# Norm sums gathered with the output blocks instead of from the updated residual, in a two-layer hybrid decoder step

## The chip, the cores and the metric

The kernel runs on one core of a Trainium2 chip. The metric is device time in microseconds (us) of one execution, as the median of several runs. The engines are named as the profile names them: PE multiplies matrices (PEld loads its weights), DVE is the vector engine, ACT the scalar engine, POOL is GpSimd, SP issues the transfers.

## The reference, cut to what matters

One inference step of two trunk layers, for 512 prompt tokens and 64 sample tokens together (576 columns). Each layer is a feed-forward network (FFN), a token mixer and a second FFN. The first layer's mixer is a state-space mixer with a gated linear unit (GLU), the second's is a latent attention. Every one of the six sublayers is wrapped by two norms:

```python
def rms_norm(x, g):
    y = x * rsqrt(mean(x * x, axis=-1, keepdims=True) + 1e-6)
    return y * g

h = f(rms_norm(x, norm_pre))            # f: FFN, state-space mixer or attention
x = x + w * rms_norm(h, norm_post)      # w is 1/2 for an FFN, 1 for a mixer
```

So the norm in front of a sublayer needs the sum of squares of an x that the norm behind the sublayer before has just changed. Width is 1024, the FFN's inner width 2816, everything is float32.

## The kernel before, in words

Activations stand transposed: 128 partitions by 8 blocks k of the width, by 576 columns in two halves h of 288 (`hs(h)`). X is the residual, Y the output of a sublayer, R the factor of the norm in front (one number per column, spread over all partitions), ACC the sum of squares by partition. A product is done with operands split in a high and a low part, three matmuls per pair (`mm3`, L155 to L158); weights are split on ACT and DVE as they land (`split`, L149; `load`, L174); `xsplit` (L189) makes XH and XL from X for a sublayer's first product.

`stats` (L98) sums ACC over partitions on PE (L103), works out the inverse root in nine small operations on DVE (L107 to L116) and builds a diagonal `rs_d` (L117). `spread` (L124) multiplies it by ones on PE (L127), so that the factor stands on all partitions. `post` (L205) adds the normed output to X, block by block: one operation on DVE to make t, one addition on DVE or POOL, then `xsplit`. `squares` (L232) then takes the squares of the new X on ACT and adds them up on POOL.

`tail` (L247) is the end of every sublayer. Blocks 6 and 7 of half 0 are computed, half 0's output norm is worked out while block 6 of half 1 runs, and half 0's residual while block 7 of half 1 runs. Half 1's norm and residual are left in `state["pend"]`, and `first_units` (L262) of the next sublayer runs them between its matmuls: norm after k = 0, residual after k = 2. Then it sums ACC for half 0 (L275) and half 1 (L287) and spreads both into R; R is needed when the first products leave PSUM (`evac`).

The state-space mixer (`s5_mixer`, L622) has no such first product. It starts with `run_pend` (L645): all of half 1's residual, the squares of half 1 (L222 to L227), both norms D0 and D1. Then a pipeline of ten steps over eight blocks k follows: `s_u` scales X[:, k] by R into `un`, `s_a` and `s_b` transpose, `s_c` and `s_s` run the recurrence on products kept in pieces of Y (`wk`), `s_d` and `s_e` make the output. `zeros` (L649) clears some buffers on POOL, tied behind the last residual addition (L812).

The order within an engine is set before the run by a planner: it takes the instruction that comes first in the program among those it believes ready, by its own costs, and `issue_after` ties one behind another. Buffers are rings: "t1" has four, "sq" three.

Of the kernel before, what the change touches and what calls it, by code (L numbers as in the profile page):

```python
# [9 lines left out]
F32 = mybir.dt.float32  # L10
# [7 lines left out]
T = 576  # L18
# [7 lines left out]
def build(nc, tc, a, subs=(0, 1, 2, 3, 4, 5)):  # L26
# [9 lines left out]
    with ctx:  # L36
# [40 lines left out]
        ACC = cst.tile([128, T], F32, name="ACC")  # L77
        GP = cst.tile([128, 6, 2, 8], F32, name="GP")
# [19 lines left out]
        def stats(accs, col=None, scale=1.0, eps=1e-6):  # L98

            src = psum()[:CP, :4]  # L100
            for i, z in enumerate(accs):
                for j in range(4):
                    P.matmul(src[:, j:j + 1], z[:, j * CP:j * CP + CP], ones[:, 0:1] if col is None else col,  # L103
                             start=i == 0 and j == 0, stop=i == len(accs) - 1 and j == 3)
            q, t, y = [cur["sm"].tile([CP, 4], F32, name=nm) for nm in ("rs_a", "rs_t", "rs_y")]

            V.tensor_scalar(q, src, eps, None, op0=OP.add)  # L107
# [8 lines left out]
            V.scalar_tensor_tensor(y, t, 5.0, y, op0=OP.add, op1=OP.mult)  # L116
            d = smt("rs_d")[:CP]  # L117
            state["y"] = y
# [3 lines left out]
            return d  # L122

# [8 lines left out]
        def sqacc(acc, src, first, scale=1.0, defer=False, ve=False, add=None):  # L132
            if ve:
                sq = acc if first else smt("sq")
                V.tensor_tensor(sq, src, src, op=OP.mult)
                if not first:
                    G.tensor_tensor(acc, acc, sq, op=OP.add)
                return None
            if first:
                A.activation(acc, src, AF.Square, scale=scale)  # L140
                return None
            sq = sqd.tile([128, H], F32, name="sqd") if defer else smt("sq")
            ins = A.activation(sq, src, AF.Square, scale=scale)  # L143
            if defer:
                state["sqd"] = ins
                return sq
            (add or G).tensor_tensor(acc, acc, sq, op=OP.add)  # L147
# [56 lines left out]

        def post(n, h, rs, nxt):  # L205
            last = None
            for k in range(8):
                t = smt("t1")
                V.scalar_tensor_tensor(t, Y[:, k, hs(h)], GP[:, n, 1, k:k + 1], rs, op0=OP.mult, op1=OP.mult)  # L209
                ve = k % 2 if nxt in (None, 1) else k % 4 == 0  # L210
                ins = (V if ve else G).tensor_tensor(X[:, k, hs(h)], X[:, k, hs(h)], t, op=OP.add)  # L211
                last = last if ve else ins
                if nxt is None:
                    if k % 2:
                        S.dma_start(a["o_y"][:, k - 1:k + 1, hs(h)], X[:, k - 1:k + 1, hs(h)])
                elif nxt != 1:
                    xsplit(nxt, h, k)
            if nxt == 1 and h == 1:
                state["add"] = last
                s5["D0"] = stats([ACC[:, hs(0)]]), state["y"]  # L220
                sqs = []
                for k in range(8):  # L222
                    sqs.append(s5["sq"].tile([128, H], F32, name="sq%d" % k))
                    A.activation(sqs[k], X[:, k, hs(h)], AF.Square)
                for x, y in ((4, 5), (6, 7), (4, 6)):
                    V.tensor_tensor(sqs[x], sqs[x], sqs[y], op=OP.add)
                s5["D1"] = stats(sqs[:5]), state["y"]  # L227
            elif h == 1:
                squares(h, nxt, last)
            return last  # L230

        def squares(h, nxt, last):  # L232
            if nxt is not None:
                with tc.issue_after(last.ins), tc.issue_after(state["sqd"].ins):
                    for k in range(8):
                        sqacc(ACC[:, hs(h)], X[:, k, hs(h)], k == 0, add=G)

# [9 lines left out]
        def tail(n, blk, mlast, SQ, nxt):  # L247

            for m in mlast:
                blk(m, 0)  # L250
            d0 = stats([ACC[:, hs(0)], SQ[0]])
            blk(mlast[0], 1)
            if nxt not in (None, 1):
                state["W0"] = cur["load"](first(nxt, 0), 2048)
            last = post(n, 0, spread(d0), nxt)
            for m in mlast[1:]:
                blk(m, 1)
            squares(0, nxt, last)
            d1 = []
            state["pend"] = [lambda: d1.append(stats([ACC[:, hs(1)], SQ[1]])), lambda: post(n, 1, spread(d1[0]), nxt)]  # L260

        def first_units(W, evac, K=8):  # L262
# [12 lines left out]
            d0 = stats([ACC[:, hs(0)]])  # L275
            qq = [[], []]
            for u in range(2):
                for g in range(2):
                    qq[u].append(psum()[:, :H])
                    for k in range(K):  # L280
                        mmk(u, qq[u][g], 1, g, k)
                    if (u, g) == (0, 0):
                        spread(d0, R[:, hs(0)])
                        for v in range(2):
                            evac(v, 0, pp[v])
                    if (u, g) == (0, 1):
                        d1 = stats([ACC[:, hs(1)]])  # L287
            spread(d1, R[:, hs(1)])
# [14 lines left out]
        def ffn(i, n, nxt, tick=lambda *z: None):  # L303
# [7 lines left out]
            def evac(f, h, pp):  # L311
                t, s, u = smt("t1"), smt("t2"), smt("t3")
                V.tensor_tensor(t, pp[0], R[:, hs(h)], op=OP.mult)  # L313
                A.activation(s, t, AF.Silu)  # L314
                V.tensor_tensor(u, pp[1], R[:, hs(h)], op=OP.mult)  # L315
                g = G.tensor_tensor(u, u, s, op=OP.mult)  # L316
                tick(*split(HH[:, f, hs(h)], HL[:, f, hs(h)], u), g)

            if n == subs[0]:
# [9 lines left out]
                d0 = stats([ACC[:, hs(0)]])  # L329
# [3 lines left out]
                d1 = stats([ACC[:, hs(1)]])  # L333
# [19 lines left out]
            for s in range(2):  # L353
# [5 lines left out]
                def down(d, h):  # L359
# [6 lines left out]
                    if s == 0:  # L366
                        tick(A.activation(y, o, AF.Copy))
                    else:
                        ins = V.tensor_tensor(y, o, y, op=OP.add)  # L369
                        SQ[h] = sqacc(ACC[:, hs(h)], y, d == 0, defer=d == 7)  # L370
                        tick(ins)
# [250 lines left out]
        def s5_mixer(n, nxt, es_c):  # L622
# [13 lines left out]
            if n == subs[0]:  # L636
# [4 lines left out]
                for h in range(2):  # L641
                    s5["D%d" % h] = stats([ACC[:, hs(h)]]), state["y"]
            es_q = ExitStack()
            s5["sq"] = mkpool(es_q, "s5q", 1, reuse_waits="tile")
            run_pend()  # L645
            es_q.close()
# [11 lines left out]
            wk = lambda k, i: fl[:, (4 * (k % 2) + i) * 512:(4 * (k % 2) + i) * 512 + 512].rearrange("p (r g c) -> p r g c", r=2, g=4)  # L658
            UN, U2, WVt, RTt, TTt, YTt, MKt = {}, {}, {}, {}, {}, {}, {}

            def s_u(k):
# [6 lines left out]
                if k:  # L668
                    V.scalar_tensor_tensor(u, X[:, k], GP[:, n, 0, k:k + 1], R, op0=OP.mult, op1=OP.mult)
# [11 lines left out]
            def s_a(k):  # L681

                TT = TTt[k] = ep.tile([CP, 8, 8, 16], F32, name="TT")
                if k == 0:

                    u = UN[0]
                    for h in range(2):
# [77 lines left out]
            def s_e(k):  # L765
# [3 lines left out]
                for h in range(2):  # L769
# [3 lines left out]
                    y, w, sq = smt("t2"), smt("t3"), smt("sq")  # L773
# [22 lines left out]
            for s in range(10):  # L796
# [11 lines left out]
                if s == 0:  # L808
# [4 lines left out]
                    with tc.issue_after(state["add"].ins) if "add" in state else nullcontext():  # L813
                        zeros()
# [31 lines left out]
            def gevac(m, h, pp):  # L846
# [4 lines left out]
                SQ[h] = sqacc(ACC[:, hs(h)], y, m == 0, scale=0.5, defer=m == 7)  # L851
# [28 lines left out]
        def mla(n, nxt):  # L880
# [77 lines left out]
            for h in range(2):  # L958
                t, u = smt("t1")[:64], smt("t2")[:32]
# [104 lines left out]
            for u in range(6):  # L1064
# [5 lines left out]
                for h in range(2):  # L1070
# [3 lines left out]
                    if u < 2:  # L1074
                        t = [smt(nm) for nm in ("t1", "t2", "t3", "sq")]
# [67 lines left out]
            def evac(m, h, o):  # L1143
                A.activation(Y[:, m, hs(h)], o, AF.Copy)
                SQ[h] = sqacc(ACC[:, hs(h)], Y[:, m, hs(h)], m == 0, defer=m == 7)
# [14 lines left out]
            for m in range(2, 6):  # L1160
                for h in range(2):
                    blk(m, h)
# [393 lines left out]
```

## Time and profile before

| what | value |
|---|---|
| median of 3 runs | 2486.22 us (2485.14 to 2488.54) |
| profiled execution | 2486.95 us, span of its instructions 2485.2 us |
| PE busy | 2381.8 us, 96% of the span |
| DVE busy | 1281.5 us, 52% |
| ACT busy | 873.6 us, 35% |
| POOL busy | 556.1 us, 22% |
| mean granted clock of PE | 0.978 of 2.4 GHz |
| chain that ended last | PE 68%, DVE 6%, ACT 2%, POOL 1% |

Busy time is the union of an engine's instructions. The rows in a later section are of four kinds. A row of the waits names who waited, for whom, the us in total, how often, and the longest. A timeline row has the start in us from the span's start, the duration, the engine, the line of the kernel, the operation, output and inputs, shape, how many were merged, and in brackets the idle time before it and who ended it. A row of groups (lines) has busy us, the mean in ns, and idle us before. A row of windows has busy us (and number) for each engine in a stretch.

### The profile page before, as it was taken

The page shows a single profiled execution, that of the slowest core. Times are in us where ns is not written, and L with a number is a line of the kernel's source. Part 1 is how long each engine was busy: PE and PEld are TensorE (multiplying, and loading weights), DVE is VectorE, ACT ScalarE, POOL GpSimd, SP SyncE. Part 2 cuts the span into 40 slices and gives each one's busy share as a digit, 9 for nine tenths or more (in the row PEclk, how much of TensorE's full clock was granted, in tenths as well). Part 3 has the DMA queues.
Part 4 walks back from the last instruction along what each step waited for, and adds up shares of the span by engine and source line. Part 5 has one row for each costly group of instructions (what it writes and reads, how often), then busy time and mean ns, then how long its engine had stood idle before and what let it go on. Part 6 is the DMA issues. An engine that isn't in the chain of part 4 may idle for free.

```text
span 2485.2 us, 44160 instructions
## 1 busy us (share of the span) xinstructions
PE 2381.8 (96%) x17610; PEld 2313.1 (93%) x17610; DVE 1281.5 (52%) x2647; ACT 873.6 (35%) x1807; POOL 556.1 (22%) x819
## 2 busy tenths in 40 slices
PE   7999999789989999998999999899999999999998
PEld 7999999679989999998999999798888898999997
DVE  7564565685464233347432433767777655423434
ACT  4222322353332222224222222434666653222221
POOL 3123535452231001124100112530000042100112
PEclk9999999799989999998999999999999999999999
DMA  3224343473212222222223222345555332222221
GB/s 126 86 86 146 126 130 118 125 188 97 77 60 86 71 92 86 75 88 68 80 67 101 86 70 76 114 114 178 169 173 179 130 104 69 75 74 99 86 71 63
DMA packets 114642, 254.89 MB, mean 103 GB/s; under 512 B 25122, under 2 KB 53539, under 8 KB 114179
## 3 DMA queue, kind: packets, MB, share of 16 engines
q1 hardware_dynamic: 114434, 252.06, 32.0%
q8 instruction: 139, 2.28, 0.4%
q14 instruction: 69, 0.56, 0.1%
HBM read 231.79 MB, written 22.59 MB: 102 GB/s over the span
## 4 chain that ended last, share of the span: by engine, by line
PE 68%; DVE 6%; ACT 2%; issue 1%; POOL 1%; DMA 1%; SPq 0%; ACTq 0%; DVEq 0%; POOLq 0%
PE ps L158 20%; PE ps L156 20%; PE ps L157 20%; PE ps L1331 2%; PE ps L1296 2%; DVE XHL L153 1%; DVE t L209 1%; POOL X L211 1%; PE ps L127 1%; PE ps L1237 1%; DVE wlo L151 1%; PE ps L1317 0%; PE ps L757 0%; PE ps L1225 0%; ACT Pm L1198 0%
## 5 line engine op out<-in xcount | busy, mean ns | idle before, releaser
L156 PE MATMUL ps<-XHL,whi 128*128 128x288 f32 x3344 | 1002.4, 300 | 20.4 <-ACT whi L151 12.9
L157 PE MATMUL ps<-XHL,whi 128*128 128x288 f32 x3344 | 998.7, 299 | 4.7 <-DVE XHL L153 4.7
L158 PE MATMUL ps<-XHL,wlo 128*128 128x288 f32 x3344 | 995.9, 298 | 1.4 <-DVE wlo L151 1.4
L156 PEld LDWEIGHTS ps<-XHL,whi 128*128 128x128 f32 x3344 | 638.2, 191 | 24.3 <-ACT whi L151 13.5
L157 PEld LDWEIGHTS ps<-XHL,whi 128*128 128x128 f32 x3344 | 639.0, 191 | 9.6 <-DVE XHL L153 7.4
L158 PEld LDWEIGHTS ps<-XHL,wlo 128*128 128x128 f32 x3344 | 637.9, 191 | 2.2 <-DVE wlo L151 2.0
L151 DVE TENSOR_TENSOR wlo<-raw,whi 128x1024 fp32r<-128x1024 f32 (+2 forms) x349 | 409.3, 1198 | 317.3 <-ACT whi L151 316.6
L151 ACT ACTIVATE whi<-raw 128x1024 fp32r<-128x1024 f32 (+2 forms) x349 | 321.6, 946 | 446.0 <-PE ps L157 378.2
L158 PE MATMUL ps<-HH,wlo 128*128 128x288 f32 x1408 | 415.8, 296 | 1.9 <-DVE wlo L151 1.9
L156 PE MATMUL ps<-HH,whi 128*128 128x288 f32 x1408 | 417.3, 296 | 0.0
L157 PE MATMUL ps<-HL,whi 128*128 128x288 f32 x1408 | 415.3, 295 | 0.0
L316 POOL TENSOR_TENSOR t<-t,t 128x288 f32<-128x288 f32 x176 | 143.1, 813 | 1113.2 <-DVE t L315 983.5
L158 PEld LDWEIGHTS ps<-HH,wlo 128*128 128x128 f32 x1408 | 265.2, 188 | 2.6 <-DVE wlo L151 2.6
L156 PEld LDWEIGHTS ps<-HH,whi 128*128 128x128 f32 x1408 | 265.3, 188 | 0.4
L157 PEld LDWEIGHTS ps<-HL,whi 128*128 128x128 f32 x1408 | 265.3, 188 | 0.2
L315 DVE TENSOR_TENSOR t<-ps,R 128x288 f32<-128x288 f32 x176 | 80.2, 456 | 331.3 <-PE ps L158 331.1
L147 POOL TENSOR_TENSOR ACC<-ACC,sq 128x288 f32<-128x288 f32 x137 | 138.3, 1010 | 391.2 <-ACT sq L143 387.0
L314 ACT ACTIVATE t<-t 128x288 f32<-128x288 f32 x176 | 77.9, 444 | 329.6 <-DVE t L313 313.2
L151 ACT ACTIVATE HH<-t 128x288 fp32r<-128x288 f32 x176 | 77.2, 439 | 249.0 <-POOL t L316 242.2
L151 DVE TENSOR_TENSOR HL<-t,HH 128x288 fp32r<-128x288 f32 x176 | 81.7, 465 | 125.2 <-ACT HH L151 124.8
L313 DVE TENSOR_TENSOR t<-ps,R 128x288 f32<-128x288 f32 x176 | 79.3, 450 | 53.8 <-PE ps L158 47.9
L369 DVE TENSOR_TENSOR Y<-ps,Y 128x288 f32<-128x288 f32 x64 | 29.2, 455 | 129.4 <-PE ps L158 129.4
(332 smaller groups left out, 2612.9 us busy)
## 6 DMA issues: line engine op xcount, KB each, us to landing
raw<-GU SPq DMA_DIRECT2D x176, 512.0 KB, 4.1
pgr<-PG SPq DMA_DIRECT2D x128, 320.0 KB, 3.5
raw<-DN SPq DMA_DIRECT2D x64, 512.0 KB, 3.5
raw<-DN SPq DMA_DIRECT2D x64, 192.0 KB, 3.4
raw<-GLU SPq DMA_DIRECT2D x16, 512.0 KB, 4.2
CAd<-s5w SPq DMA_DIRECT2D x8, 576.0 KB, 3.6
WVd<-s5w SPq DMA_DIRECT2D x8, 512.0 KB, 3.4
wv<-WVd SPq DMA_DIRECT2D x8, 512.0 KB, 5.8
```

What stands on the lines that cost most here:

```text
L147: (add or G).tensor_tensor(acc, acc, sq, op=OP.add)
L151: return A.activation(hi, src, AF.Copy), V.tensor_tensor(lo, src, hi.bitcast(F32), op=OP.subtract)
L156: P.matmul(o, wh, xh, start=st, stop=False)
L157: P.matmul(o, wh, xl, start=False, stop=False)
L158: P.matmul(o, wl, xh, start=False, stop=sp)
L313: V.tensor_tensor(t, pp[0], R[:, hs(h)], op=OP.mult)
L314: A.activation(s, t, AF.Silu)
L315: V.tensor_tensor(u, pp[1], R[:, hs(h)], op=OP.mult)
L316: g = G.tensor_tensor(u, u, s, op=OP.mult)
L369: ins = V.tensor_tensor(y, o, y, op=OP.add)
L1296: P.matmul(so, qb[:, cb], d["kv"][u][:, :, 256 + cb * 128:384 + cb * 128], start=cb == 0, stop=False)
L1331: P.matmul(o, d["pt"][:, c], d["kv"][i // 2][:, i % 2, 0:256], start=i == 0, stop=i == 3)
```

## The change

Let a be the factor of the output norm per column, g its gain and y the output. Then the sum over the new x of (x + a g y)² is sum x² + 2a sum xgy + a² sum (gy)². The changed kernel carries sum x² in SA (72 columns on partitions, by half and group) and gathers three sums with every output block (`ymom`): y² in ACC, x·g·y in R, (g·y)² in a new ACQ. `mom_a` sums them over partitions and gives the output norm, `mom_b` updates SA and gives the next norm. `squares` is gone, and so are the two sums in `first_units`; R of half 0 is spread at the end of `tail`, R of half 1 after half 1's residual. In the attention's output product blocks 0 and 1 gather their sums only when block 2 begins, since X comes back from memory there.

In the state-space mixer, half 1's norm is worked out first and spread into ACC; block k of its residual (`post1`) is done in `s_a(0)` and `s_u(k)`, inside the pipeline. As Y must live until then, the products' buffers `wk` use fewer pieces of Y, ACQ and one new tile. `zeros` is not tied any more. "t2" is dropped, and "t1" serves for it (the gate's SiLU is done in place).

```diff
-        def stats(accs, col=None, scale=1.0, eps=1e-6):
+        def mom_a(h, SQ):
+            src = sums([[ACC[:, hs(h)], SQ[h][0]]])
+            bc = sums([[R[:, hs(h)], SQ[h][1]], [ACQ[:, hs(h)], SQ[h][2]]])
+            q = cur["sm"].tile([CP, 4], F32, name="rs_a")
+            V.tensor_scalar(q, src, 1e-6, None, op0=OP.add)
+            y = rsqrt(q)
+            return y, bc
+
+        def mom_b(h, y, bc):
+            m = cur["sm"].tile([CP, 4], F32, name="rs_m")
+            V.tensor_tensor(m, bc[:, 4:8], y, op=OP.mult)
+            V.scalar_tensor_tensor(m, bc[:, 0:4], 2.0, m, op0=OP.mult, op1=OP.add)
+            V.tensor_tensor(m, m, y, op=OP.mult)
+            V.tensor_tensor(SA[:, h], SA[:, h], m, op=OP.add)
+            V.tensor_scalar(SA[:, h], SA[:, h], 0.0, None, op0=OP.max)
+            q = cur["sm"].tile([CP, 4], F32, name="rs_ab")
+            V.tensor_scalar(q, SA[:, h], 1e-6, None, op0=OP.add)
+            y2 = rsqrt(q, "b")
+            return diag(y2, tag="b"), y2
+
+        def ymom(n, m, h, y, sc=1.0):
+            g = GP[:, n, 1, m:m + 1]
+            out = []
+            for i, acc in enumerate((ACC, R, ACQ)):
+                dst = acc[:, hs(h)] if m == 0 else (smt("t1") if i else sqd.tile([128, H], F32, name="sqd")) if m == 7 else smt("sq")
+                if i == 1:
+                    V.scalar_tensor_tensor(dst, y, g, X[:, m, hs(h)], op0=OP.mult, op1=OP.mult)
+                else:
+                    A.activation(dst, y, AF.Square, scale=g if i else sc)
+                if 0 < m < 7:
+                    G.tensor_tensor(acc[:, hs(h)], acc[:, hs(h)], dst, op=OP.add)
+                out.append(dst)
+            return out
...
-        def squares(h, nxt, last):
-            if nxt is not None:
-                with tc.issue_after(last.ins), tc.issue_after(state["sqd"].ins):
-                    for k in range(8):
-                        sqacc(ACC[:, hs(h)], X[:, k, hs(h)], k == 0, add=G)
...
             for m in mlast:
                 blk(m, 0)
-            d0 = stats([ACC[:, hs(0)], SQ[0]])
+            y0, bc0 = mom_a(0, SQ)
+            d0 = diag(y0)
             blk(mlast[0], 1)
...
-            squares(0, nxt, last)
-            d1 = []
-            state["pend"] = [lambda: d1.append(stats([ACC[:, hs(1)], SQ[1]])), lambda: post(n, 1, spread(d1[0]), nxt)]
+            if nxt == 1:
+                s5["D0"] = mom_b(0, y0, bc0)
+
+                def half1():
+                    y1, bc1 = mom_a(1, SQ)
+                    d1 = diag(y1)
+                    s5["D1"] = mom_b(1, y1, bc1)
+                    spread(d1, ACC[:, hs(1)])
+                    s5["post"] = lambda k: post1(n, 1, ACC[:, hs(1)], nxt, k)
+                state["pend"] = [half1]
+                return
+            if nxt is not None:
+                spread(mom_b(0, y0, bc0)[0], R[:, hs(0)])
+            z = {}
+
+            def norm1():
+                z["y"], z["bc"] = mom_a(1, SQ)
+                z["d"] = diag(z["y"])
+
+            def rest1():
+                post(n, 1, spread(z["d"]), nxt)
+                if nxt is not None:
+                    spread(mom_b(1, z["y"], z["bc"])[0], R[:, hs(1)])
+            state["pend"] = [norm1, rest1]
...
-            d0 = stats([ACC[:, hs(0)]])
             qq = [[], []]
...
-                        spread(d0, R[:, hs(0)])
...
-                    if (u, g) == (0, 1):
-                        d1 = stats([ACC[:, hs(1)]])
-            spread(d1, R[:, hs(1)])
...
                 if k:
+                    s5["post"](k)
                     V.scalar_tensor_tensor(u, X[:, k], GP[:, n, 0, k:k + 1], R, op0=OP.mult, op1=OP.mult)
...
-                    with tc.issue_after(state["add"].ins) if "add" in state else nullcontext():
-                        zeros()
+                    zeros()
```

## Rows read from the trace of the kernel before

**Rows 1.** The page, busy us, share of the span and instructions of PE.
```profile
PE 2381.8 (96%) x17610; PEld 2313.1 (93%) x17610; DVE 1281.5 (52%) x2647; ACT 873.6 (35%) x1807; POOL 556.1 (22%) x819
```
**Rows 2.** Waits of PE, whole span: us in total, times, longest.
```profile
PE ps L127 <- DVE rs_d L119: 35.2, 13, 4.8
```
**Rows 3.** Waits of PE, stretches 655 to 710 and 1960 to 2070.
```profile
PE ps L127 <- DVE rs_d L119: 5.8, 2, 3.8
...
PE ps L127 <- DVE rs_d L119: 6.3, 2, 4.0
```
**Rows 4.** Timeline of PE, 1128 to 1149, between the two FFNs.
```profile
1130.26 0.66 PE L127 MATMUL ps<-rs_d,ones 72*128 72x288 f32 x1 [1.86 <-DVE rs_d L119]
...
1146.87 1.30 PE L127 MATMUL ps<-rs_d,ones 72*128 72x288 f32 x2 [3.70 <-DVE rs_d L119]
```
**Rows 5.** Timeline of PE, 1104 to 1111.
```profile
1104.41 0.62 PE L103 MATMUL ps<-ones,ACC 128*72 128x1 f32 x8
1104.89 0.38 PE L156 MATMUL ps<-HH,whi 128*128 128x288 f32 x1
...
1109.89 0.65 PE L127 MATMUL ps<-rs_d,ones 72*128 72x288 f32 x2
```
**Rows 6.** Timeline of DVE, then POOL, 1105 to 1150.
```profile
1106.69 0.16 DVE L107 TENSOR_SCALAR rs_a<-ps 72x4 f32<-72x4 f32 x1 [1.62 <-PE ps L103]
...
1108.43 0.45 DVE L119 SCALAR_TENSOR_TENSOR rs_d<-ident,rs_y 72x288 f32<-72x288 f32 x1
1110.09 0.46 DVE L369 TENSOR_TENSOR Y<-ps,Y 128x288 f32<-128x288 f32 x1 [1.20 <-PE ps L158]
...
1125.62 0.14 DVE L107 TENSOR_SCALAR rs_a<-ps 72x4 f32<-72x4 f32 x1
...
1129.26 0.94 DVE L119 SCALAR_TENSOR_TENSOR rs_d<-ident,rs_y 72x288 f32<-72x288 f32 x1
...
1124.71 7.01 POOL L147 TENSOR_TENSOR ACC<-ACC,sq 128x288 f32<-128x288 f32 x7 [2.82 <-ACT sq L143]
```
**Rows 7.** Timeline of PE, ACT, POOL and DVE, 458 to 485, start of the mixer.
```profile
458.47 0.62 PE L103 MATMUL ps<-ones,ACC 128*72 128x1 f32 x8
460.74 0.68 PE L103 MATMUL ps<-ones,sqd 128*72 128x1 f32 x8 [1.65 <-ACT sqd L143]
...
480.77 1.22 PE L711 MATMUL ps<-ident,TT 72*128 72x72 f32 x8 [4.14 <-ACT TT L694]
...
483.94 0.51 PE L723 MATMUL ps<-U,wv 128*64 128x72 f32 x4
...
479.59 1.12 ACT L694 ACTIVATE TT<-ps,rs_y 72x128 f32<-72x128 f32 x4 [1.24 <-DVE rs_y L116]
...
472.44 3.96 POOL L656 MEMSET CKb<- 64x1024 f32 x4
...
473.62 0.92 DVE L688 TENSOR_SCALAR un<-X,GP 128x288 f32<-128x288 f32 x1
```
**Rows 8.** Windows, then timeline of DVE and POOL, 510 to 520, inside the mixer.
```profile
510.00:520.00 10.00, 9.20 (x95) 7.58 (x94) 9.59 (x19) 5.85 (x16) 5.96 (x7) 1.00 0.87 227
...
516.69 0.28 DVE L778 TENSOR_SCALAR t<-sq 128x288 f32<-128x288 f32 x1
...
518.71 1.37 DVE L778 TENSOR_SCALAR t<-sq 128x288 f32<-128x288 f32 x1
...
518.13 1.78 POOL L739 TENSOR_TENSOR Y<-Y,rt 128x512 f32<-128x512 f32 x1
```
**Rows 9.** Attention's output product: transfer of X (landing us), groups of POOL.
```profile
X<-XD SPq DMA_DIRECT2D x1, 2304.0 KB, 12.4
...
L147 POOL TENSOR_TENSOR ACC<-ACC,sq 128x288 f32<-128x288 f32 x7 | 6.4, 920 | 15.2 <-ACT sq L143 15.2
```
**Rows 10.** Groups of PE, 2470 to the end.
```profile
L127 PE MATMUL ps<-rs_d,ones 72*128 72x288 f32 x2 | 1.3, 750 | 2.3 <-DVE rs_d L119 2.3
```

More of the change, by code (lines that the diff above doesn't have):

```diff
@@ L95, in smt, with sums, rsqrt @@
             return cur["sm"].tile([128, w], dt, name=name, **(dict(bufs={"t1": 4, "sq": 3}[name]) if name in ("t1", "sq") else k))
-        def stats(accs, col=None, scale=1.0, eps=1e-6):
-            src = psum()[:CP, :4]
-            for i, z in enumerate(accs):
+        def sums(groups, col=None):
+            src = psum()[:CP, :4 * len(groups)]
+            lst = [(z, g) for i in range(max(map(len, groups))) for g, q in enumerate(groups) for z in q[i:i + 1]]
+            for i, (z, g) in enumerate(lst):
                 for j in range(4):
[L103 to L107, printed above, removed]
+                    P.matmul(src[:, 4 * g + j:4 * g + j + 1], z[:, j * CP:j * CP + CP], ones[:, 0:1] if col is None else col,
+                             start=i == 0 and j == 0, stop=i == len(lst) - 1 and j == 3)
+            return src
+        def rsqrt(q, tag="a"):
+            t, y = [cur["sm"].tile([CP, 4], F32, name=nm + tag) for nm in ("rs_t", "rs_y")]
             V.tensor_scalar(y.bitcast(I32), q.bitcast(I32), -0.5, float(0x5F1FFFF9), op0=OP.mult, op1=OP.add)
@@ L130, in spread, with sqacc @@
             A.activation(out, pp, AF.Copy)
[L132 removed]
+        def sqacc(acc, src, first, ve=False):
             if ve:
@@ L139, in sqacc @@
             if first:
-                A.activation(acc, src, AF.Square, scale=scale)
+                A.activation(acc, src, AF.Square)
                 return None
[L142 to L147, printed above, removed]
+            sq = smt("sq")
+            A.activation(sq, src, AF.Square)
+            G.tensor_tensor(acc, acc, sq, op=OP.add)
         def split(hi, lo, src, g=None):
@@ L203, in xsq, with post1 @@
                     sqacc(ACC[:, hs(h)], X[:, k, hs(h)], k == 0, ve=True)
+        def post1(n, h, rs, nxt, k):
+            t = smt("t1")
+            V.scalar_tensor_tensor(t, Y[:, k, hs(h)], GP[:, n, 1, k:k + 1], rs, op0=OP.mult, op1=OP.mult)
+            ve = k % 2 if nxt in (None, 1) else k % 4 == 0
+            (V if ve else G).tensor_tensor(X[:, k, hs(h)], X[:, k, hs(h)], t, op=OP.add)
+            if nxt is None:
+                if k % 2:
+                    S.dma_start(a["o_y"][:, k - 1:k + 1, hs(h)], X[:, k - 1:k + 1, hs(h)])
+            elif nxt != 1:
+                xsplit(nxt, h, k)
         def post(n, h, rs, nxt):
-            last = None
             for k in range(8):
[L208 to L221, printed above, removed]
-                for k in range(8):
[L223 to L230, printed above, removed]
-        def squares(h, nxt, last):
-            if nxt is not None:
-                with tc.issue_after(last.ins), tc.issue_after(state["sqd"].ins):
-                    for k in range(8):
-                        sqacc(ACC[:, hs(h)], X[:, k, hs(h)], k == 0, add=G)
+                post1(n, h, rs, nxt, k)
         def first(n, u):
@@ L686, in s_a @@
                     u = UN[0]
+                    s5["post"](0)
                     for h in range(2):
@@ L1161, in mla @@
                 for h in range(2):
+                    if m == 2:
+                        for z in range(2):
+                            ymom(n, z, h, Y[:, z, hs(h)])
                     blk(m, h)
```

45 lines of the change are left out of this document (26 added, 19 removed).

## The prediction

> **What bounds the kernel now.** I read busy shares first. PE is busy 96% of the span [rows 1], VectorE (DVE) and GpSimd (POOL) far less; nothing off PE can buy more than PE's gaps. So the second view is PE's waits. Of its named waits the largest by far is the spread of a norm (L127) behind the diagonal rs_d that VectorE builds: 35.2 us in 13 times [rows 2]; weights at stage starts and the split activations XHL come far behind. The third view asks where: each of the four passages from one sublayer to the next (from 660, 1100, 1545, 2018 us on) holds 5.5 to 6.3 us of that one wait, with one piece of 3.8, 3.7, 3.9 and 4.0 (the first and the last of the four rows stand in [rows 3]). That piece is the sum over the new x: after the first product of half 1 PE stands 3.70 us, until 1146.87, for the spread of R [rows 4]. The fifth passage, into the state-space mixer, is another case: 25.5 us from the last down projection's sums (458.47) to the first L723 (483.94), mostly waiting [rows 7].
>
> The changed kernel knows the new norm without x: sum(x²)+2a·sum(xgy)+a²·sum((gy)²), so R no longer waits for the residual.
>
> **One ordinary passage, part by part (there are four).**
> Removed: the long wait, mean 3.85 us [rows 3, 4], and the slow spread after it, 1.30 us [rows 4]. A spread of R is still issued, but among other matmuls, where one takes 0.65 [rows 5]. Net -(3.85+1.30-0.65) = -4.5.
> Removed: two sums over x² (L103, 4 sums, 8 records). One pushes the next product matmul back from 1104.41 to 1104.89: 0.48 us [rows 5]. Two: -0.96.
> Added: `mom_a` sums four more accumulators per half, 4 x 0.48 = 1.92 us. Half 0's stand in the dense stream of the last blocks: +1.92. Half 1's can run where PE stands 1.86 us for the first spread [rows 4]: 0, at most +1.92.
> Moved: the VectorE chain that frees half 1's residual. Alone it takes from 1106.69 to the end of rs_d, 2.2 us; in the passage 4.6 us (1125.62 to 1130.20), beside POOL's seven x² additions, 7.01 us; its diagonal lasts 0.94 instead of 0.45 [rows 6]. Those additions are gone from there: -2.4. Against it +0.46 for xgy of the last block on DVE (taken as the evacuation's, as many columns), and `mom_b`: 6+8 small operations at 0.193 (one every 1.74/9 in the free chain) and a diagonal of 0.45, 3.2 us per half. For half 0 I put it at nothing: after its diagonal at 1108.9 DVE has no work until the evacuation at 1110.1 (1.20 idle), and PE's extra 1.92 lengthens that hole to 3.1 us. Without this cover it is +3.2: from 1110 to 1125 DVE's queue carries residual, splits and weights. For half 1 it is behind the residual, and R of half 1 is needed only by the last evacuations of the first units. I take -1.5 of the -2.4+0.46 = -1.9.
> What is late next: the split XHL of half 1, which today ends before the x² chain of half 1 can start, some 5 us ahead of 1146.87 (a chain of 4.6 lies between), and then a little earlier; PE goes on from there without stopping for R.
> Sum: -4.5-0.96+1.92-1.5 = -5.0, between -5.9 (whole -2.4) and +2.0 (-4.5-0.96+1.92+1.92+3.2+0.46). Times four: **-20 us**, -24 to +8.
>
> **Into the state-space mixer.** Today half 1's chain and residual, then the x² of half 1, then its chain stand in line. Afterwards: Y and squares 2.3 us (458.47 to 460.74), sums 0.7, four extra accumulators 1.9 at full and up to 4 at half clock, `mom_b` 3.2, TT 1.1, then as now 3.2 from L711 (480.77) to L723: 12.4 to 14.5, I take 14 [rows 7]. Beside `mom_b` run a spread (1.30 at most [rows 4]), block 0's residual (0.46, and an addition of 0.92 [rows 9]) and transposes: 4 or less with its bc sums, no longer than that path. Saved 25.5-14 = 11.5; half 0's extra sums cost 1.92 in front: -9.6.
> Given back: blocks 1 to 7 of half 1's residual now sit in `s_u`, inside the pipeline. There DVE, not PE, is the bound: 9.59 of 10.00 us busy [rows 8]. Each k adds one t and each odd k an X addition on DVE, both as the 0.46 of [rows 6]: 7x0.46+4x0.46 = +5.0. The even X additions go to POOL, and DVE pays beside POOL: L778 takes 0.28 alone and 1.37 beside L739 of 1.78 [rows 8], 1.1 lost in 1.78; three additions of 0.92 cost 0 to 3x0.6, I take +1.2. The ring of product buffers (Y no longer free) shares Z between steps, which are 10 us apart: 0.
> `zeros()` loses its edge behind the last addition, so its 4 us of memsets may run beside the norm's chain. Today they run at 472.44 to 476.4, and a scaling of 288 columns, L688, took 0.92 there [rows 7], while L778, as wide, takes 0.28 alone [rows 8]. From nothing to the 2.4 that POOL's additions cost a chain; I take +0.5, one such loss, as these two rows lie nearest.
> The Trainium skill ("SBUF — State Buffer", Who interferes with whom) says that DVE and GpSimd hold a shared port pair exclusively, and that a two-input DVE operation is blocked only by a GpSimd operation that reads SBUF. By it memsets would stop only the chain's few TENSOR_SCALARs, and the value would be nearer 0.5 than 2.4; by it too each even X addition can block DVE for its whole length, 3x0.92 = 2.8 instead of 1.2. The trace of before agrees as far as L778 and L688 go, and holds no residual addition inside this pipeline.
> Sum: -9.6+6.2+0.5 = **-3 us**, -9 (half of the DVE work hidden by waits of the opening steps, faster start) to +3.
>
> **Everywhere else.** Each half block before a passage gets one more square on ACT, one xgy (0.46) on DVE and two more POOL additions of 0.92 [rows 9]. They lie beside PE: at one matmul in 0.133 us (33 in the 4.4 of a down projection) 48 are 6.4 us, 24 in the attention's output product 3.2. Only there is POOL tight: 3x0.92 = 2.8 of 3.2. X, now needed early, lands 12.4 us after its issue behind the first weights [rows 9], and the first four products (96 matmuls) last 12.8. The 33 additions that half 0's sums need are 30.4 us at 0.92 and 33.0 at the 1.00 of [rows 6]; PE's ten half blocks between are 32. The three squares' buffers tie ACT and DVE to POOL there. I take **+1** (0 to 4). The mixed t1/t2 buffers: 0, four are enough for one evacuation at a time.
> The last sublayer has no successor but computes the sums: half 0's 1.92 stand among matmuls; half 1's lie beside the 2.3 us for which PE waits for rs_d [rows 10]: **+2**.
>
> Total -20-3+1+2 = -20. The profiled execution took 2486.95 us (span 2485.2 and 1.75 around it), 0.7 above the median of the three runs shown, 2486.22. Against the median: **2466 us**.
>
> **Rivals.**
> *The wait changes its name (no change).* R comes early but half 1's XHL comes as late as R did, because `mom_b` and xgy stand in DVE's queue ahead of the splits. Then the 4.5 stay away only in name: -0.96+1.92 per passage, +4, end +2, others +1, mixer -3, and the first chain's -1.5 x 4: 2484. For: DVE feeds all of these. Against: today a whole chain of 4.6 us lies between the last split and R [rows 4, 6].
> *DVE becomes the bound (slower).* If both `mom_b` chains of a passage stand in front of residual and split, XHL is 6.4 us later per passage: -4.5-0.96+1.92+6.4+0.46 = +3.3, four times +13; with the mixer at +1 and end and rest at +3: 2503. It decides where more than some 3 of these 6.4 us stand ahead of the splits. For: a list order by priority is fixed before the run. Against: the residual precedes `mom_b` in the program.
> *The mixer keeps its whole gain and passages also stop waiting at the first spread:* -24-9+2 = -31, 2455. For: only a stretch in the mixer's middle was read as full. Against: 9.59 of 10 there.
> That the norm is not early after all would need `mom_b` to be queued behind post of both halves: this is the first rival.
>
> **How the numbers follow.** Forecast 0.58 (own range 2458 to 2478), larger gain 0.17, wait renamed 0.14, slower 0.11. 0.2% is 5 us, about what a measurement of this kernel tells from none. Faster (under 2481): the first two and 0.02 of the renamed wait, which lies 3 us above that edge, 0.77; within 0.2% the rest of it, 0.12; slower 0.11. The range 2447 to 2484 covers the larger gain and the renamed wait, and leaves out the slower case and a tail below.
>
> **What would show it.** Right: no wait of 3.7 us for rs_d after the first product of half 1, four passages of about 46 instead of 51 us; L723 some 10 us after where it stood relative to its tail; steps of the mixer of 10.6 to 11 instead of 10.1 us. Wrong: PE waiting over 5 us for XHL in the passages, DVE busy without a hole from the last block to half 1's splits, POOL still adding in the output product when half 0's sums are due.

## The result, and the profile after

The changed kernel takes 2561.48 us (median of four runs, 2544.24 to 2563.72) where the kernel before took 2486.63 beside it: ratio 1.0284, 95% interval 1.0262 to 1.0306. The forecast was 2466 (2447 to 2484), so the sign is wrong. The profiled execution took 2563.22 us, its span 2561.5 us.

The page of the changed kernel, first its busy times: PE is 95% busy, 40 us more than in [rows 1]. Sums are added, and more products run at the lower clock, where they start every 0.24 us instead of every 0.13 (second passage, 1128 to 1131 us and 1133 to 1137 us).
```profile
PE 2421.4 (95%) x17882; PEld 2357.3 (92%) x17882; DVE 1333.1 (52%) x2792; ACT 885.9 (35%) x1824; POOL 636.0 (25%) x900
```
Waits of PE, whole span (us in total, times, longest). Lines have moved: on PE, L181 is the spread that was L127, L106 the sums that were L103, and L207 to L209 the product matmuls that were L156 to L158; on DVE, L127 is the diagonal that was L119. The wait that was to shrink from 35.2 us [rows 2] has doubled.
```profile
PE ps L181 <- DVE rs_d L127: 71.4, 12, 13.5
...
PE ps L209 <- DVE wlo L202: 8.6, 7, 3.3
PE ps L106 <- POOL ACC L174: 4.0, 1, 4.0
```
The same wait in the first two passages (655 to 730, 1100 to 1185), against 5.8 us in two pieces in the first passage before [rows 3]:
```profile
PE ps L181 <- DVE rs_d L127: 10.9, 1, 10.9
...
PE ps L181 <- DVE rs_d L127: 16.7, 2, 13.4
```
The first passage differs from the other three. Half 0's whole chain ran there ahead of the residual, as forecast (its diagonal on DVE ends at 677.09), and its spread on PE (685.12) waits for nothing. The 10.95 us are those of half 1's R.
```profile
676.64 0.45 DVE L127 SCALAR_TENSOR_TENSOR rs_d<-ident,rs_yb 72x288 f32<-72x288 f32 x1
...
685.12 0.65 PE L181 MATMUL ps<-rs_d,ones 72*128 72x288 f32 x2
...
720.43 0.85 PE L181 MATMUL ps<-rs_d,ones 72*128 72x288 f32 x1 [10.95 <-DVE rs_d L127]
```
Timeline of PE in the second passage (start, us, idle before and its releaser), answering to [rows 4]. The last block ends at 1137.5. Then PE stands 13.41 us, spreads R of half 0, and only then issues the first product over XHL. A second stand, of 3.30 us, comes at half 1's R. The third and fourth passage have the same two stands, 13.49 and 3.31, 13.40 and 3.31.
```profile
1137.24 0.29 PE L209 MATMUL ps<-HH,wlo 128*128 128x288 f32 x1
1150.94 1.33 PE L181 MATMUL ps<-rs_d,ones 72*128 72x288 f32 x2 [13.41 <-DVE rs_d L127]
1151.65 0.85 PE L207 MATMUL ps<-XHL,whi 128*128 128x288 f32 x1
...
1178.27 0.48 PE L181 MATMUL ps<-rs_d,ones 72*128 72x288 f32 x1 [3.30 <-DVE rs_d L127]
```
Timeline of DVE there, answering to [rows 6]: ten of the fourteen small operations of `mom_b(0)` run by 1129.2, as forecast. Then DVE idles 3.47 us, because the next instruction in its queue is the evacuation L420 (a block's product moved out of PSUM), and PE has not finished that block. The last four (L118 to L121) stand behind it, and three of them and the diagonal (L127) also behind half 0's whole residual (L259, L261), its splits (L204) and the low halves of weights (L202).
```profile
1129.06 0.16 DVE L117 SCALAR_TENSOR_TENSOR rs_yb<-rs_tb,rs_yb 72x4 f32<-72x4 f32 x1
1132.69 0.46 DVE L420 TENSOR_TENSOR Y<-ps,Y 128x288 f32<-128x288 f32 x1 [3.47 <-PE ps L209]
1133.06 0.15 DVE L118 SCALAR_TENSOR_TENSOR rs_tb<-rs_yb 72x4 f32<-72x4 f32 x1
1133.18 0.52 DVE L259 SCALAR_TENSOR_TENSOR t<-Y,GP,ps 128x288 f32<-128x288 f32 x1
...
1137.91 1.04 DVE L204 SCALAR_TENSOR_TENSOR XHL<-X,GP,XHL 128x288 fp32r<-128x288 f32 x1
...
1147.41 0.14 DVE L119 TENSOR_TENSOR rs_tb<-rs_tb,rs_ab 72x4 f32<-72x4 f32 x1
1147.48 1.21 DVE L202 TENSOR_TENSOR wlo<-raw,whi 128x1024 fp32r<-128x1024 f32 x1
...
1150.43 0.46 DVE L127 SCALAR_TENSOR_TENSOR rs_d<-ident,rs_yb 72x288 f32<-72x288 f32 x1
```
Windows of PE's stretches around the stand (window, length, busy us of PE, PEld, DVE, ACT, POOL, granted clock, DMA): after it the clock is at its lower level, 1.2 GHz, nearly throughout. By an estimate from the granted 0.52 these 16 us of work lose up to 16 x (1 - 0.52) = 7.7 us more.
```profile
1125.00:1137.00 12.00, 12.00 (x74) 11.89 (x74) 7.76 (x27) 3.31 (x5) 2.98 (x3) 0.72 0.07 18
...
1151.00:1167.00 16.00, 16.00 (x89) 15.60 (x90) 3.80 (x22) 0.41 (x1) 0.00 (x0) 0.52 0.13 47
```
Ahead of the mixer and at its start (PE), answering to [rows 7]: a weight half comes 3.25 us late, and the first state product (L773) starts 19.6 us after half 1's sums (467.34 to 486.95) instead of 25.5.
```profile
434.04 0.40 PE L209 MATMUL ps<-HH,wlo 128*128 128x288 f32 x1 [3.25 <-DVE wlo L202]
...
470.96 0.28 PE L106 MATMUL ps<-ones,sqd 128*72 128x1 f32 x1 [1.96 <-ACT sqd L172]
...
483.79 0.38 PE L761 MATMUL ps<-ident,TT 72*128 72x72 f32 x1 [2.89 <-ACT TT L744]
...
486.95 0.39 PE L773 MATMUL ps<-U,wv 128*64 128x72 f32 x2
```
DVE there: `mom_b(1)` begins at 475.63 and ends with its diagonal at 483.08; operations of the residual stand among its own.
```profile
476.59 0.17 DVE L159 TENSOR_SCALAR rs_ab<-SA 72x4 f32<-72x4 f32 x1
477.65 0.52 DVE L259 SCALAR_TENSOR_TENSOR t<-Y,GP,ACC 128x288 f32<-128x288 f32 x1 [0.89 <-ACT ACC L184]
478.08 0.16 DVE L113 TENSOR_SCALAR rs_yb<-rs_ab 72x4 int32<-72x4 int32 x1
...
482.62 0.46 DVE L127 SCALAR_TENSOR_TENSOR rs_d<-ident,rs_yb 72x288 f32<-72x288 f32 x1
```
The attention's output product (POOL and DVE, then PE), answering to [rows 9]: an addition takes 0.81 us beside DVE's product x·g·y (L170), but 1.79 where the split of a weight (L202) has begun before it, and half 0's sums wait for the last of them.
```profile
2068.07 0.81 POOL L174 TENSOR_TENSOR ACQ<-ACQ,sq 128x288 f32<-128x288 f32 x1
2068.14 1.05 DVE L170 SCALAR_TENSOR_TENSOR sq<-Y,GP,X 128x288 f32<-128x288 f32 x1 [1.47 <-POOL R L174]
...
2070.43 1.29 DVE L202 TENSOR_TENSOR wlo<-raw,whi 128x1024 fp32r<-128x1024 f32 x1 [1.24 <-ACT whi L202]
2070.60 1.79 POOL L174 TENSOR_TENSOR ACQ<-ACQ,sq 128x288 f32<-128x288 f32 x1
...
2076.86 0.23 PE L106 MATMUL ps<-ones,ACC 128*72 128x1 f32 x1 [3.99 <-POOL ACC L174]
```
The end (PE): the last spread starts 6.8 us after half 1's first sums (2544.72), against 4.9 in the kernel before (2470.34 to 2475.28).
```profile
2551.54 1.33 PE L181 MATMUL ps<-rs_d,ones 72*128 72x288 f32 x2 [0.37 <-DVE rs_d L127]
```

**Where the time went.** All these kernels issue the same 15,024 product matmuls, in the same order but for stretches inside the passages, none of which holds a row of this table. So the start of the n-th in two traces tells how late one kernel is at that place. Differences to the kernel before, in us, from the profiled executions (e1, b1 and m1 are runs told below; e1's profiled execution is the fastest of its four, 8.0 us under its median):
```
product at                            before    after     e1      b1      m1
2900  first sublayer, last blocks     418.60    +0.8    +0.9    -0.5    +0.7
3167  last ahead of the mixer         458.34    +8.9   +10.3   +10.6    +0.3
3168  first behind the mixer          562.51    +8.6    +4.5    +7.7    +1.1
4300  behind passage 1                741.44   +17.6    +1.9    +6.7    -1.6
7400  behind passage 2               1173.66   +33.3    -5.5    -0.6    -8.9
10500 behind passage 3               1607.22   +46.3   -11.3    -9.0   -14.8
11700 attention's output product     2008.28   +50.2   -12.6    -7.4   -15.7
11820 half 0's sums there            2025.34   +60.3    -2.2    -2.1   -10.6
12200 behind passage 4               2094.42   +72.4    -3.9   -10.6   -19.3
15023 last product                   2470.20   +74.4    +1.1   -10.7   -19.4
```
Column "after": 9.0, 15.6, 13.0 and 12.1 us in the four passages, 8.9 ahead of the mixer, 3.9 in the attention ahead of its output product, 10.2 in that product, 2.0 to the last product; the end of the span adds 1.9. Of the 3.9 us in the attention 3.0 are one wait that the change did not bring (last section).

### The profile page after: what moved, and what is told of

Read it like the earlier page. It is cut to its first block, busy times and chain, and to the rows that moved or that the text cites. A ratio compares the mean times of both kernels' runs of the same rounds, so it can differ in the third digit from the quotient of the medians.

```text
span 2561.5 us, 44898 instructions
## 1 busy us (share of the span) xinstructions
PE 2421.4 (95%) x17882; PEld 2357.3 (92%) x17882; DVE 1333.1 (52%) x2792; ACT 885.9 (35%) x1824; POOL 636.0 (25%) x900
## 5 line engine op out<-in xcount | busy, mean ns | idle before, releaser
L207 PE MATMUL ps<-XHL,whi 128*128 128x288 f32 x3344 | 1003.4, 300 | 14.5 <-ACT whi L202 13.6
L209 PE MATMUL ps<-XHL,wlo 128*128 128x288 f32 x3344 | 995.6, 298 | 1.4 <-DVE wlo L202 1.4
L207 PEld LDWEIGHTS ps<-XHL,whi 128*128 128x128 f32 x3344 | 638.2, 191 | 16.4 <-ACT whi L202 13.9
L209 PEld LDWEIGHTS ps<-XHL,wlo 128*128 128x128 f32 x3344 | 636.9, 191 | 2.0 <-DVE wlo L202 2.0
L202 DVE TENSOR_TENSOR wlo<-raw,whi 128x1024 fp32r<-128x1024 f32 (+2 forms) x349 | 417.2, 1220 | 279.0 <-ACT whi L202 278.4
L202 ACT ACTIVATE whi<-raw 128x1024 fp32r<-128x1024 f32 (+2 forms) x349 | 321.8, 946 | 428.3 <-PE ps L208 358.5
L209 PE MATMUL ps<-HH,wlo 128*128 128x288 f32 x1408 | 417.8, 297 | 7.2 <-DVE wlo L202 7.2
L207 PE MATMUL ps<-HH,whi 128*128 128x288 f32 x1408 | 418.3, 297 | 0.0
L209 PEld LDWEIGHTS ps<-HH,wlo 128*128 128x128 f32 x1408 | 266.3, 189 | 8.4 <-DVE wlo L202 8.4
L207 PEld LDWEIGHTS ps<-HH,whi 128*128 128x128 f32 x1408 | 266.3, 189 | 0.4
L202 ACT ACTIVATE HH<-t 128x288 fp32r<-128x288 f32 x176 | 77.0, 438 | 240.0 <-POOL t L367 233.4
L174 POOL TENSOR_TENSOR ACC<-ACC,sq 128x288 f32<-128x288 f32 x72 | 85.1, 1181 | 268.3 <-ACT sq L172 268.3
L202 DVE TENSOR_TENSOR HL<-t,HH 128x288 fp32r<-128x288 f32 x176 | 80.9, 459 | 125.0 <-ACT HH L202 124.6
L181 PE MATMUL ps<-rs_d,ones 72*128 72x288 f32 x56 | 24.7, 533 | 71.4 <-DVE rs_d L127 71.4
```

The source lines that it names most:

```text
L174: G.tensor_tensor(acc[:, hs(h)], acc[:, hs(h)], dst, op=OP.add)
L202: return A.activation(hi, src, AF.Copy), V.tensor_tensor(lo, src, hi.bitcast(F32), op=OP.subtract)
L207: P.matmul(o, wh, xh, start=st, stop=False)
L209: P.matmul(o, wl, xh, start=False, stop=sp)
```

## The experiments

Theory A: the loss is the place of R's spreads in PE's queue. Half 0's stands ahead of the first products over XHL and waits for a chain that DVE ends only behind the residual; the products have their data and stand behind it. Theory A2: the rest is the load of the new accumulators on ACT, DVE and POOL, in two stages (ahead of the mixer, the attention's output product) and at the end. Rivals B to F are named in the expectations. The expectation of e1 puts all four long waits down to half 0's R; the first of them (10.95) is half 1's, as shown above.

**e1**, the spreads where the kernel before has them; the arithmetic is the same:
```
-                spread(mom_b(0, y0, bc0)[0], R[:, hs(0)])
+                y2 = mom_b(0, y0, bc0, False)[1]
...
                 z["d"] = diag(z["y"])
+                if nxt is not None:
+                    state["R0"] = diag(y2)
...
-                    spread(mom_b(1, z["y"], z["bc"])[0], R[:, hs(1)])
+                    state["R1"] = mom_b(1, z["y"], z["bc"])[0]
...
                     if (u, g) == (0, 0):
+                        spread(state.pop("R0"), R[:, hs(0)])
...
+            spread(state.pop("R1"), R[:, hs(1)])
             evac(0, 1, qq[0])
```


> The spreads of R are issued on TensorE where the kernel before issues them (half 0's after the first unit of half 1, half 1's behind the last first unit), and half 0's diagonal behind the diagonal of half 1's first norm; all the arithmetic stays. Theory A (TensorE's queue: the spread of R(0) stands ahead of the first XHL products and waits for a chain that VectorE ends only behind half 0's residual): the waits of 11 to 13.5 us for rs_d, 51.3 us in four passages, and the 3.3 us waits for half 1's R (9.9 us) go; a few us of waits for XHL come in their place (1 to 3 per passage, as in the kernel before); with less half-rate clock behind them the time falls from 2561 to 2485-2505 us. Rival B (VectorE is the bound of the passage, as the prediction's slower case had it: the split XHL itself comes late): the waits only change their name to XHL, 10 us or more in each passage, and the time stays above 2540 us.

Measured: 2497.74 us (2489.75 to 2505.54), ratio to before 1.0057 [1.0036, 1.0078]. Waits of PE from 1095 to 1165 in e1, and its timeline:
```profile
PE ps L207 <- ACT XHL L204: 1.9, 3, 0.9
PE ps L208 <- DVE XHL L204: 1.3, 1, 1.3
```
```profile
1139.69 0.41 PE L181 MATMUL ps<-rs_d,ones 72*128 72x288 f32 x1
...
1153.91 0.41 PE L181 MATMUL ps<-rs_d,ones 72*128 72x288 f32 x1
```
The spreads at 1139.69 and 1153.91 wait for nothing, and XHL costs 3.2 us where rs_d cost 16.7. DVE's chain still ends late (the diagonal at 1133.63, 14.9 us after the last block's end); it no longer matters. Theory A holds: the place of the spreads costs 64 us. Rival B, DVE as the bound, falls.

**e2**, the other end of the same wait: half 0's spread stays, and its chain is put ahead on DVE: the residual is tied behind the chain's diagonal (`state["dg"]`).
```
-            post(n, 0, spread(d0), nxt)
...
+                r0 = mom_b(0, y0, bc0)[0]
+                with tc.issue_after(state["dg"].ins):
+                    post(n, 0, spread(d0), nxt)
...
-                spread(mom_b(0, y0, bc0)[0], R[:, hs(0)])
+                spread(r0, R[:, hs(0)])
```


> The spread of R(0) keeps its place ahead of the first XHL products on TensorE, but on VectorE half 0's chain of the next norm is put ahead of half 0's residual (the residual's instructions are ordered behind that chain's diagonal). Theory A: the four waits of 11 to 13.5 us go, because rs_d is ready some 4 us behind the first norm's chain; the residual, and with it XHL, starts 1 to 3 us later; the 3.3 us waits for half 1's R stay; 2495-2520 us. Rival B (VectorE is the bound, both chains ahead of residual and splits make it worse): XHL is late by as much as the chain takes and by the weight splits, TensorE waits over 8 us for XHL in each passage, above 2540 us.

Measured: 2546.69 us, 1.0249 [1.0230, 1.0268], so the number I gave for A (2495 to 2520) missed. Timeline of PE in e2, second passage:
```profile
1136.43 0.41 PE L181 MATMUL ps<-rs_d,ones 72*128 72x288 f32 x1
1138.95 0.40 PE L207 MATMUL ps<-XHL,whi 128*128 128x288 f32 x1 [1.87 <-ACT XHL L204]
...
1169.70 0.85 PE L181 MATMUL ps<-rs_d,ones 72*128 72x288 f32 x1 [11.76 <-DVE rs_d L127]
```
Half 0's stand is gone, as A says, and XHL costs 1.87, not B's 8. But half 1's R does the same thing one step later: its spread stands ahead of remaining products, its chain behind half 1's residual, and PE stands 10.95, 11.76, 12.20 and 10.56 us for it in the four passages. In the changed kernel's second passage twelve of that chain's fourteen operations had run before half 1's residual (to 1163.13), so it showed as 3.30 only; in its first passage, where PE does not stand for half 0, four had, and the stand is 10.95 there too.

**e4** tests that reading: e2, and half 1's spread late as in e1.

> As e2 (half 0's chain of the next norm ahead of its residual on VectorE), and the spread of half 1's R issued behind the last first unit. e2 removed half 0's wait (the first XHL product of the passage from 1100 us ran at 1138.95 instead of 1151.65) but then stood 11.8 us for half 1's R, whose spread stands ahead of half 0's later units and waits for a chain behind half 1's residual. Theory A (TensorE's queue, twice): the four waits of about 12 us go, 45 us or more with the half-rate clock behind them, 2490-2505 us as e1. Rival B (VectorE bound): half 1's XHL is late in their place, above 2525 us.

Measured: 2491.22 us (2486.39 to 2507.11, ten runs), 1.0016 [1.0003, 1.0029]. As A says: with e2's remedy for half 0 the late place for half 1 is needed too, and gives 55 us. (The late place for half 0 alone was not run.)

**e3 and e5** leave out the accumulators' work (`for i, acc in enumerate((ACC,))` in `ymom`, the sums reading ACC's tiles thrice), without and with e1's edit. They show what that work costs in time; both compute less than the reference.

> Leaves out the two new accumulators' squares, products and additions (the sums read ACC's tiles three times instead, so that TensorE's sums, both chains and every place in the queues stay). Theory A: the four waits of 11 to 13.5 us for rs_d stay as they are, since nothing in the order changes; only what the load of the accumulators costs goes: the late weight halves ahead of the mixer (6 us), the wait for POOL's ACC in the attention's output product (4 us) and some of the end, so 2535-2553 us. Rival C (the added load on ScalarE, VectorE and GpSimd is what delays the passages): the waits for rs_d shrink below 6 us and the time falls under 2515 us.

> e1 (spreads of R late on TensorE) and leaves out the two new accumulators' squares, products and additions as in e3 (the sums and chains stay). What the load of the accumulators costs once no spread is in the way. Theory A2 (POOL and VectorE late in two stages, ahead of the mixer and in the attention's output product, beside the end): 6 to 11 us ahead of the mixer and 8 in the output product go, 2470-2482 us. Rival D (the load lies beside TensorE, as the prediction had it, at +1 to +4): 2490-2497 us.

Measured: e3 2525.31 us, 1.0161 [1.0144, 1.0178]; e5 2462.31, 0.9892 [0.9875, 0.9908]. Both gain more than A2 gave them, 36 and 35 us. In e3 the waits for rs_d stay (58.6 us in 11 times), so C falls; the gain beyond the two stages is 5 to 6 us in each passage, where the stand for half 0 is 10.9 to 11.5 us instead of 13.4. D falls: the load costs 35 us, not 4. Together: 64 us for the place and 35 for the load, less the 25 that e5 lies below the kernel before, are 74 of the 75 us.

**b1** is e1 with a third of POOL's additions on DVE in the attention sublayer, and no moments in the last sublayer.
```
-            for i, acc in enumerate((ACC, R, ACQ)):
+            for i, acc in enumerate((ACC, R, ACQ) if n != subs[-1] else (ACC,)):
...
-                    G.tensor_tensor(acc[:, hs(h)], acc[:, hs(h)], dst, op=OP.add)
+                    (V if i == 1 and n == 4 else G).tensor_tensor(acc[:, hs(h)], acc[:, hs(h)], dst, op=OP.add)
```


> e1, with the additions of x*g*y on VectorE instead of GpSimd in the attention sublayer alone, and no moments gathered in the last sublayer. Theory A2: GpSimd is late in the output product (TensorE stands 4.0 us for ACC and runs at half rate behind it, +10 us there), so taking a third of its additions away gives 6 to 9 us; the last sublayer gives back 4 to 6: 2483-2489 us. Rival E: the additions take turns with GpSimd's on the two engines' common path (a product on VectorE takes 1.05 us beside GpSimd instead of 0.52), so nothing is won there and only the end gives back: 2491-2494 us.

Measured: 2477.23 us (2476.23 to 2486.52), 0.9969 [0.9952, 0.9985], 6 us below A2's range. PE's wait for POOL's ACC is 0.9 instead of 4.0, and from product 11700 to 12200 b1 gains 3.2 us on the kernel before where e1 loses 8.7. E falls.

**b2 and t1** are b1 with the state-space tables, prepared in the first sublayer, paced over 40 and 48 steps instead of 52 (`// 52`), to take them out of the last down projections.

> b1, with the preparation of the state-space tables paced over 40 steps instead of 52, so that it ends before the last down projections of the first sublayer, where the moments are gathered. Theory A2: ahead of the mixer VectorE and GpSimd are late because both loads meet there (weight halves 4.6 to 6 us late); taking the tables out gives 5 to 8 us against b1. Rival F: the tables then delay weight halves earlier in the sublayer by as much: within 2 us of b1.

> b1, with the tables paced over 48 steps instead of 52 (b2 had 40: ahead of the mixer it was 8 us better than b1, in the sublayer's middle 30 us worse). Theory A2: at 48 the middle costs little (0 to 3 us) and the last down projections lose less of VectorE to the tables: 2472-2479 us. Rival F (each table delays a weight half wherever it stands): 2480 us or more.

Measured: b2 2493.32 us, 1.0022 [1.0012, 1.0031]; t1 2480.44, 0.9985 [0.9972, 0.9998]. From product 2900 to 3167 b2 loses 2.7 us instead of b1's 11.1, so the two loads do collide there. But the middle of the sublayer pays 30 (9 in t1): the tables delay weight halves wherever they stand, as F has it, and in b2 by more (16 us over b1, where F gave 2). Waits of PE in b2, 190 to 415, where e1 has 1.2 us in all:
```profile
PE ps L207 <- ACT whi L202: 10.3, 3, 5.4
PE ps L647 <- DVE s5w L640: 5.2, 2, 4.7
```

**m1** is b1 with the way into the mixer as before: no moments in the first sublayer, half 1's residual as a whole, the norm from squares of the new x, whose sums `nrm` keeps in SA.
```
-                s5["D0"] = mom_b(0, y0, bc0)
...
+                    post(n, 1, spread(diag(mom_a(1, SQ)[0])), nxt)
+                    s5["D0"] = nrm([ACC[:, hs(0)]], 0)
...
-                    s5["post"](k)
```


> b1, with the way into the state-space mixer as in the kernel before: no moments in the first sublayer, the norm from squares of the new x, half 1's residual as a whole ahead of the mixer, its first sums kept for the later norms. By the trace of the changed kernel this part costs what it brings: +8.9 us ahead of the mixer (weight halves late behind the moments' work and the tables' work on VectorE, the added sums), 5.9 us earlier first step, 5.6 us given back in the steps. Theory A2: taking it back gives 6 to 10 us against b1, 2467-2472 us. The prediction's reading (the mixer part gains 3 us): 2478-2481 us.

Measured: 2468.89 us (2464.72 to 2478.02, six runs), 0.9934 [0.9919, 0.9948]: as A2 says, and the fastest of the kernels that compute the whole, 17 us below the kernel before. Windows 420 to 440 ahead of the mixer, of the changed kernel and then of m1: PE stands 4.6 us of 20 with DVE at 19.2 and POOL at 15.9, and 0.3 without the moments.
```profile
420.00:440.00 20.00, 15.42 (x113) 14.94 (x113) 19.21 (x33) 6.99 (x14) 15.89 (x12) 1.00 0.40 132
```
```profile
420.00:440.00 20.00, 19.70 (x160) 19.10 (x159) 16.97 (x37) 6.27 (x11) 8.30 (x5) 1.00 0.50 165
```

## Why the prediction was wrong

**The step that failed** is the wait for R, which the prediction had at nothing for both halves: "PE goes on from there without stopping for R". It measured 61.2 us: 40.3 for half 0 (13.41, 13.49, 13.40 in passages 2 to 4) and 20.9 for half 1 (10.95 in the first, 3.30, 3.31, 3.31), and products at the lower clock behind most of these stands; e1 takes back 64.

For half 0 the sentence was "For half 0 I put it at nothing: after its diagonal at 1108.9 DVE has no work until the evacuation at 1110.1". In the first passage that came out. In the others the hole was there, 3.47 us long even after ten of the operations had run. But the order of DVE's queue is fixed before the run, and it had the last four operations behind the evacuation and the residual. I priced the missing cover at the chain's own length, +3.2. Its price was that of everything queued ahead of it. For half 1 the sentence was that R "is needed only by the last evacuations of the first units". That says who needs it, and not where its spread stands: ahead of products that do not need it, with its chain behind half 1's residual.

The removed `spread(d0, ...)` and `spread(d1, ...)` lines of the diff show the place: R's spread of half 0 goes from behind the first unit of half 1 to ahead of the first product over XHL, that of half 1 from behind the last first unit to half 1's residual. I wrote that "A spread of R is still issued, but among other matmuls", and never asked which matmuls stand behind it.

The Trainium skill ("PSUM — Partial Sum Buffer", Engine vs sequencer instructions) says that matmuls start and complete in program order. The trace agrees: half 0's first XHL is split by 1138.95 (L204, 1137.91 and 1.04) and is multiplied at 1151.65, behind the spread.

**The four passages otherwise came out, in part by luck.** With the spreads late, passages 1 to 3 give -2.6, -7.4 and -5.8 in e1; in m1, 1 to 4 with the output product give -2.6, -7.4, -5.9 and -3.5, some -19 against my -20. The new x's wait is gone, XHL is what is late, for 3.2 us in e1's second passage. The sums of the four stretches (product 3168 to 4300, to 7400, to 10500, and 11700 to 12200; length, then busy us), of the kernel before and then of m1:
```profile
sum 1130.85, PE 1092.89 PEld 1080.19 DVE 507.28 ACT 363.48 POOL 232.91; mean PE 273.22 PEld 270.05 DVE 126.82 ACT 90.87 POOL 58.23
```
```profile
sum 1111.42, PE 1096.67 PEld 1086.07 DVE 527.50 ACT 363.06 POOL 260.39; mean PE 274.17 PEld 271.52 DVE 131.87 ACT 90.77 POOL 65.10
```
PE's idle time falls by 23.2 us; the prediction's terms for it, 4 x (3.85 + 1.5), are 21.4. PE's busy time rises by 3.8, for a forecast of 4 x (0.96 - 0.65) = 1.2. That small figure hides two errors against each other: half 1's sums stand among the products too and are not free (1.92 each, by the prediction's own price), and less work falls into the lower clock (in the second passage the granted clock goes from 0.98 to 1.00), for which the prediction had only the slow spread.

**"Everywhere else +1" was mis-sized.** In the output product I saw POOL tight (30.4 to 33.0 us of additions in 32) and still put the sum near nothing; it measured +10.2: a wait of 3.99, behind it 10.2 us at the lower clock (2077.58 to 2087.82), which lose up to half, and the added sums. An addition takes 1.8 us where the split of a weight on DVE has begun before it, in place of the 0.92 to 1.00 that I took as a mean. Ahead of the mixer I had half 0's 1.92 of sums and nothing for the load: +8.9, where moments, tables and weight halves meet on DVE.

**The mixer** was to gain 3 us. From half 1's sums to the first state product it took 19.6, not 14: the sums last until 474.0, 6.7 us, near the upper end of what I gave them, but `mom_b` on DVE lasts 7.5 (475.63 to 483.08) for my 3.2, because the residual's first blocks, which I had beside it, stand between its operations in the same queue. From the first state product (L723 before, L773 after) to product 3168 it is 84.2 us after and 78.6 before, so the steps gave back 5.6, near the 6.2 forecast. With the load ahead of it the part costs 6.6 (3168 in b1 and m1), 8 us in time.

**The end** measured +3.9 for +2: 2.0 to the last product, with half 0's sums in the stream, and 1.9 at the last spread.

**The rivals.** "The wait changes its name" comes nearest, since a norm that "is not early after all", with `mom_b` queued behind the residual, was put under it. But it named XHL as what comes late, at 2484 us. "DVE becomes the bound" (0.11) had the sign and the opposite order: the chain did not delay the residual, it stood behind it. Of the three signs of being wrong only the last showed, POOL still adding when half 0's sums are due; none of the three looked at the wait for R itself.

## What to carry to other kernels

When a change makes a value ready earlier and moves its consumer forward, price the consumer's new place in its in-order queue: what stands behind it there, and when the last instruction of the producing chain really runs on its own queue. Here the late place gave back 64 us with the same arithmetic: an early value gains nothing from an early place in a queue, and a place too early stops work that needs nothing of it. Size "beside other work" by the stage that is fullest, not by the share of the span.

## What the runs showed of the hardware

- GpSimd's addition took 0.80 us alone and 0.81 beside VectorE's product x·g·y, which itself took 1.05 instead of 0.52 (2068.07 and 2068.14). Where a weight split on VectorE had begun 0.17 us before it (2070.43), it took 1.79. The Trainium skill ("SBUF — State Buffer", Who interferes with whom) has the port pair that the two engines share as an exclusive lock; the numbers fit it.
- A TENSOR_SCALAR of 72x4 on VectorE that takes 0.15 us elsewhere lasted 4.02 us where a GpSimd memset of 3.93 us began 0.06 us behind it. In e1 the same two began 0.08 us apart, and it kept its 0.15. The rows are of the changed kernel, then of e1:
```profile
1687.28 4.02 DVE L113 TENSOR_SCALAR rs_ya<-rs_a 72x4 int32<-72x4 int32 x1
...
1687.34 3.93 POOL L1028 MEMSET Q<- 32x4608 f32 x1
```
```profile
1629.64 0.15 DVE L113 TENSOR_SCALAR rs_ya<-rs_a 72x4 int32<-72x4 int32 x1
...
1629.72 3.94 POOL L1032 MEMSET Q<- 32x4608 f32 x1
```
  It stands in the chain of a norm in the attention: PE waits 4.72 us for that spread (1694.55) instead of 1.74 before. The profiled executions of e2, e4, e5 and t1 have the long form too, those of e3, b1, b2 and m1 the short one, so it comes neither with the spreads' place nor with the moments, and 3 us between two of these profiles can be this alone.
- PE's granted clock fell to its lower level in stretches in which PE never stood, the sums in the stream of the last blocks (1125.27 to 1132.09, behind 40 records of one-column sums and 7 products), but not in every passage: at the same place e1 kept the full clock. Several kernels with these sums spread wider: the ten runs of e4 cover 20.7 us (granted clock of a run 0.973 to 0.979), of t1 17.4 and of b2 8.8, twenty runs of the kernel before 7.0. What decides it was not tried.
